# First feed-forward layer of a two-layer decoder trunk: the norm is multiplied into the inputs of later up products, and table steps run in pairs

## Chip, cores and metric

The kernel runs on one core of one Trainium2 chip. The metric is the time of one execution in device microseconds (us). Lower is better.

## What is computed

A trunk of two layers over 512 positions of width 1024, in float32. Each layer has a mixer, a cross-attention into 256 memory tokens and a gated feed-forward part. The change touches the feed-forward part of layer 0 and the tables of the state-space mixer of layer 1, which are worked out beside it. Cut to that:

```
h = rmsnorm(x, g)                       # x * rsqrt(mean(x*x)) * g
up = h @ w_up                           # (512, 1024) @ (1024, 5632)
conv = conv_b + sum_i conv_w[i] * shifted(up, i)     # 3 taps along the positions, causal
val, gate = split(conv, 2)              # 2816 channels each
x = x + (silu(gate) * val) @ w_down     # (512, 2816) @ (2816, 1024)
```

## The kernel before

Activations lie transposed: channels on the 128 partitions, the 512 positions along the free dimension. So the factor rsqrt(mean(x*x)) is one number per column; `rbc` holds it, copied to all partitions, and g is one number per partition.

**Split products.** Every float32 operand is split into a high part that TensorE takes in its faster format and the rest. A product of two operands is three matmuls (`mm3`, lines 207 to 209): high by high, low by high, high by low. The high part is a copy on ScalarE (`copy_hi`, line 113: tiles `wh`, `xh`, `hh`), the low part a subtraction on VectorE (`sub_lo`, line 116: `wl`, `hl`; line 303: `xl`).

**Weights come in chunks.** The stream `W` loads chunks of four 128x128 weight tiles, 12 matmuls each, and splits them. `W.cap[0]` is 4: the chunk in use and three that are ready. `sproj` calls `take` at the start of each chunk:

```
def take(self):
    self.cur = None
    self.fill()                       # splits one more chunk: copy_hi, sub_lo
    hi, lo, self.cur = self.ready.pop(0)
    self.fill()
    return hi, lo
```

So the call for chunk n records the split of chunk n+3, and that split stands in the queues of ScalarE and VectorE at the place in the program where chunk n is taken. Every engine works its queue in that order. The buffers `wh` and `wl` are four deep.

**The feed-forward part** (`ffn_side`) has two halves of 11 columns each. A column j is a round of two up products: the value product j and the gate product NF+j, each of 8 weight tiles, so two chunks and 24 matmuls, into a bank of PSUM named `psup`. The inputs are `xh`, `xl` without the factor `rbc`. After each product `conv` is recorded: VectorE multiplies `psup` by `rbc` into `fu` (line 1454), ScalarE makes the first tap and the bias (`fc`, line 1456), VectorE adds the other two taps (lines 1463 and 1465). After the gate product's `conv`, ScalarE applies SiLU (line 1491, the first time behind the load of its function table); in the next round VectorE multiplies value by gate (line 1460) and the result is split into `hh`, `hl`. In round 0 both convolutions are recorded behind the second product, as `rbc` has to be worked out first (`psst`, `psrow`). After 11 rounds come eight down products `psd` of 33 matmuls, each added into x.

**The table steps.** `ssm_prep` is a generator: each `next(side)` records one step, and `at(n, f)` puts f behind the step that comes n later. `conv` makes one step and each down product five (first half) or three (second half). The steps turn raw matrices on TensorE (`psrw`, four groups of 8 transposes, and `psds`), then build 16 blocks: VectorE ops `bl`, `bt` (lines 640 to 644), a group of 4 transposes `pswi` (line 217) and its copy out; then 16 blocks of `dl`, `bt` (lines 677 to 681) with a group of small float32 matmuls `psk` (line 700), copies `kt` and `wtt`, and DMAs from GpSimd's queue into `tz`. These matmuls and transposes stand between the matmuls of the big products on TensorE.

All PSUM tiles of this stage share one pool of eight banks.

Of the kernel before, what the change touches and what calls it, by code (L numbers as in the profile page):

```python
# [8 lines left out]
F32 = mybir.dt.float32  # L9
# [3 lines left out]
AF = mybir.ActivationFunctionType  # L13
ALU = mybir.AluOpType
# [4 lines left out]
KD = D // 128  # L19
DFF = 2816  # L20
NF = DFF // 128
NH = NF // 2
# [30 lines left out]
def trunk_kernel(  # L53
# [51 lines left out]
    def ttile(name, dt=F32R):  # L105
        return tp.tile([128, 512], dt, tag="t", name=name)
# [125 lines left out]
    def gcol(idx, layer, m):  # L232
        c = goff[idx] + layer * KD + m
        return gcols[:, c:c + 1]
# [335 lines left out]
    def ssm_prep_ops(rg, at):  # L570
# [29 lines left out]
        G.memset(pC[64:128, 0, :], -1.0)  # L600
        G.memset(pCi[:, 0, :], 0.0)

        dsk = rg.tile([64, 16], F32, tag="dsk", name="dsk")
        nc.gpsimd.dma_start(out=dsk, in_=ssm_d[0].rearrange("(g c) -> g c", c=16))
        tzs = [rg.tile([128, 4, 128], F32, tag=f"tz{q}", name="tz") for q in range(2)]
        for t in tzs:
# [7 lines left out]
        ps = psC("psds")  # L614
# [10 lines left out]
        at(6, lambda: cc["turn"](0))  # L625
        at(8, lambda: cc["turn"](8))
        bz = rg.tile([128, 64, 16], F32, tag="bz", name="bz")
        for b in range(2 * NB):
            gs = slice(b * 4, b * 4 + 4)
            sh = [128, 4, 16, 8]  # L630
            big, bt = (hold(n).rearrange("p a b c -> p (a b c)")[:, 0:512].rearrange("p (a b c) -> p a b c", a=4, b=16)
                       for n in ("bl", "bt"))

            def vb(t):
                return t[:, :, gs].rearrange("p c g -> p g c").unsqueeze(3).to_broadcast(sh)

            def vp(t):
                return t[:, 0:8, gs].rearrange("p m g -> p g m").unsqueeze(2).to_broadcast(sh)

            V.tensor_tensor(out=big, in0=vb(b1), in1=vp(pB), op=ALU.mult)  # L640
            yield
            V.tensor_tensor(out=bt, in0=vb(b2), in1=vp(pBi), op=ALU.mult)
            yield
            V.tensor_tensor(out=big, in0=big, in1=bt, op=ALU.add)
            st = {}

            def turn(big=big, st=st):
                st["ps"] = psC("pswi")
                for q in range(4):
                    tr(st["ps"][:, q * 128:(q + 1) * 128], big[:, q].rearrange("p c j -> p (c j)"))  # L650

            def keep(gs=gs, big=big, st=st):
                A.activation(out=bz[:, gs, :], in_=big[:, :, :, 7], func=AF.Copy)
                st["w"] = rg.tile([128, 512], F32, tag="ev", bufs=2, name="wi")
                A.activation(out=st["w"], in_=st["ps"], func=AF.Copy)

            def put(b=b, st=st):
                nc.gpsimd.dma_start(out=d_win[b // 2][:, (b % 2) * 512:(b % 2) * 512 + 512], in_=st["w"])

            at(4, turn)  # L660
            at(5, keep)
            at(6, put)
            yield

        c1, c2 = cc["d"]
        for b in range(2 * NB):
            gs = slice(b * 4, b * 4 + 4)
            sh = [128, 4, 9, 16]
            big, bt = hold("dl"), hold("bt")

            def vb(t):
                return t[:, :, gs].rearrange("p c g -> p g c").unsqueeze(2).to_broadcast(sh)

            def vp(t):
                return t[:, 0:9, gs].rearrange("p m g -> p g m").unsqueeze(3).to_broadcast(sh)

            V.tensor_tensor(out=big, in0=vb(c1), in1=vp(pC), op=ALU.mult)
            yield
            V.tensor_tensor(out=bt, in0=vb(c2), in1=vp(pCi), op=ALU.mult)
            yield  # L680
            V.tensor_tensor(out=big, in0=big, in1=bt, op=ALU.add)
            st = {}

            def d_part(d, b):
                return d[b // 2][:, (b % 2) * 512:(b % 2) * 512 + 512]

            def evw(name):
                return rg.tile([128, 4, 16, 8], F32, tag="ev", bufs=2, name=name)

            def wout(big=big, st=st):  # L690
                st["wo"] = evw("wo")
                A.activation(out=st["wo"], in_=big[:, :, 1:9, :].rearrange("p g j c -> p g c j"), func=AF.Copy)

            def put_wout(b=b, st=st):
                nc.gpsimd.dma_start(out=d_part(d_wout, b), in_=st["wo"].rearrange("p a b c -> p (a b c)"))

            def taps(b=b, big=big, st=st):
                st["ps"] = psC("psk")
                for q in range(4):
                    T.matmul(st["ps"][0:16, q * 128:(q + 1) * 128], lhsT=bz[:, b * 4 + q, :],  # L700
                             rhs=big[:, q, 0:8, :], start=True, stop=True)

            def keep(st=st):
                st["kt"] = rg.tile([16, 4, 8, 16], F32, tag="kt", bufs=1, name="kt")
                A.activation(out=st["kt"].rearrange("p a b c -> p (a b c)"), in_=st["ps"][0:16, :], func=AF.Copy)

            def spread(b=b, gs=gs, st=st):
                kt = st["kt"]
                dd = rg.tile([16, 4, 16], F32, tag="dd", bufs=2, name="dd")
                G.tensor_tensor(out=dd, in0=ident[0:16, 0:16].unsqueeze(1).to_broadcast([16, 4, 16]),  # L710
                                in1=dcol[:, gs].unsqueeze(2).to_broadcast([16, 4, 16]), op=ALU.mult)
                G.tensor_tensor(out=kt[:, :, 0, :], in0=kt[:, :, 0, :], in1=dd, op=ALU.add)  # L712
                ktf = kt.rearrange("p g t c -> p g (t c)")
                for j in range(8):
                    nc.gpsimd.dma_start(out=tzs[b % 2][j:128:8, :, j * 16:128], in_=ktf[:, :, 0:128 - j * 16])  # L715

            def band(b=b, st=st):
                st["wt"] = evw("wtt")
                A.activation(out=st["wt"], in_=tzs[b % 2].rearrange("p g (j c) -> p g c j", j=8), func=AF.Copy)

            def put_band(b=b, st=st):
                nc.gpsimd.dma_start(out=d_part(d_t, b), in_=st["wt"].rearrange("p a b c -> p (a b c)"))

            for n, f in ((2, wout), (3, taps), (3, put_wout), (4, keep), (4, spread), (9, band), (10, put_band)):
                at(n, f)
            yield

# [716 lines left out]
    def ffn_side(rg, layer, norm, hid_extra, nxt, side):  # L1444
# [4 lines left out]
        st = {"n": 0}  # L1449
        wait = {}  # L1450

        def conv(t, ps):
            u = rg.tile([128, 512], F32, tag="fu", bufs=2, name="fu")
            V.tensor_tensor(out=u, in0=ps, in1=st["rbc"], op=ALU.mult)  # L1454
            c = rg.tile([128, 512], F32, tag="fc", bufs=3, name="fc")
            A.activation(out=c, in_=u, func=AF.Identity, scale=cwcol(layer, 2, t), bias=cbcol(layer, t))  # L1456
            gate = wait.pop("gate", None)
            if gate:
                cv, cg, hl = gate
                V.tensor_tensor(out=cv, in0=cv, in1=cg, op=ALU.mult)  # L1460
                copy_hi(hl[0], cv)
            next(side, None)
            V.scalar_tensor_tensor(out=c[:, 1:], in0=u[:, :511], scalar=cwcol(layer, 1, t), in1=c[:, 1:],
                                   op0=ALU.mult, op1=ALU.add)
            V.scalar_tensor_tensor(out=c[:, 2:], in0=u[:, :510], scalar=cwcol(layer, 0, t), in1=c[:, 2:],
                                   op0=ALU.mult, op1=ALU.add)
            if gate:
                sub_lo(hl[1], cv, hl[0])
            return c

        def up(t):
            ps = psB("psup")
            sproj(ps, acts)
            if "rc" not in st:
                st["rc"] = norm.stats_cols()
                st["first"] = ps
                return None
            if "rbc" not in st:
                st["rbc"] = norm_row(st["rc"], 4)
            return ps  # L1480

        for hf in range(2):
            hid = []
            for j in range(hf * NH, (hf + 1) * NH):
                ps = up(j)
                cv = conv(j, ps) if ps is not None else None
                ps = up(NF + j)
                if cv is None:
                    cv = conv(j, st.pop("first"))
                cg = conv(NF + j, ps)  # L1490
                A.activation(out=cg, in_=cg, func=AF.Silu)
                hl = []
                for nm in ("hh", "hl"):
                    if st["n"] % 12 < hid_extra:
                        hl.append(rg.tile([128, 512], F32R, tag="hx", bufs=2 * hid_extra, name=nm))
                    else:
                        hl.append(ttile(nm))
                st["n"] += 1
                hid.append(hl)
                wait["gate"] = (cv, cg, hl)  # L1500
# [352 lines left out]
```

## Time and profile before

| | |
|---|---|
| time, median of 3 runs | 1504.48 us (1503.38 to 1505.69) |
| the profiled execution's own time | 1504.7 us |
| its span, first to last instruction | 1502.9 us |
| mean granted TensorE clock | 0.995 of full speed |
| busy share of the span: TensorE matmul | 99% |
| VectorE, ScalarE, GpSimd | 69%, 49%, 26% |

The profiled execution is one run: 1.8 us of its time lie outside its span, and it stands 0.2 us above the median. Busy matmuls are pipelined: one that is shown as 0.39 us long is followed by the next one 0.23 us later, so what a stage costs TensorE is read from starts, not from durations. The layer-0 feed-forward part runs from 385.7 to about 779.6 us.

### The profile page before, as it was taken

The numbers are of one execution on the slowest core, as the hardware profiler recorded it, in microseconds if no ns is written. First come the engines' busy times: TensorE is split into PE (matmuls) and PEld (weight loads), VectorE is DVE, ScalarE is ACT, GpSimd is POOL, SyncE is SP. The second block draws the span as 40 slices with busy tenths as digits, with TensorE's granted clock in tenths as the row PEclk, the third lists the DMA queues.
The fourth block names the chain that finished last, engine by engine and source line by source line (L and its number), as shares of the span: only waits on it lengthen the run. The fifth ranks groups of instructions, "written<-read, shape, count | busy, mean of one in ns | idle before, by whom it ended". The sixth has DMA issues, their size and how long they took to land.

```text
span 1502.9 us, 21036 instructions
## 1 busy us (share of the span) xinstructions
PE 1480.7 (99%) x7347; PEld 1234.6 (82%) x7347; DVE 1029.8 (69%) x1607; ACT 735.1 (49%) x1303; POOL 394.8 (26%) x823
## 2 busy tenths in 40 slices
PE   9999999999999999999999999999999999999998
PEld 7887888888888887888788988888888888888887
DVE  4776676676588897888865666556567775377755
ACT  5566673344445534555663545434444443245533
POOL 7864119998000013333752120000000000000002
PEclk9999999999999999999999999999999999999999
DMA  5313253324433344444568876332133333333331
GB/s 182 97 46 101 64 155 103 114 85 123 115 100 99 115 151 142 127 122 132 157 192 306 263 250 190 105 99 70 57 91 92 99 95 94 100 98 98 94 117 56
DMA packets 271941, 183.99 MB, mean 122 GB/s; under 512 B 21271, under 2 KB 252763, under 8 KB 271835
## 3 DMA queue, kind: packets, MB, share of 16 engines
q1 hardware_dynamic: 244731, 132.79, 30.2%
q0 software_dynamic: 15872, 42.26, 8.3%
q10 hardware_dynamic: 11232, 7.61, 1.6%
q8 instruction: 57, 0.93, 0.3%
q14 instruction: 49, 0.40, 0.1%
HBM read 156.13 MB, written 24.12 MB: 120 GB/s over the span
## 4 chain that ended last, share of the span: by engine, by line
PE 86%; DVE 5%; ACT 3%; DMA 2%; issue 2%; SPq 0%; ACTq 0%; POOL 0%; DVEq 0%; POOLq 0%
PE psup L207 10%; PE psup L208 10%; PE psup L209 10%; PE psd L207 5%; PE psd L209 5%; PE psd L208 5%; PE pso L209 2%; PE pso L208 2%; PE pso L207 2%; PE psg L208 2%; PE psg L207 2%; PE psg L209 2%; PE psq L207 2%; PE psq L209 2%; PE psq L208 2%
## 5 line engine op out<-in xcount | busy, mean ns | idle before, releaser
L116 DVE TENSOR_TENSOR wl<-wr,wh 128x512 fp32r<-128x512 f32 (+2 forms) x467 | 325.6, 713 | 141.6 <-ACT wh L113 140.7
L113 ACT ACTIVATE wh<-wr 128x512 fp32r<-128x512 f32 (+2 forms) x467 | 280.7, 617 | 248.3 <-PE psup L208 84.6
L207 PE MATMUL psup<-xh,wh 128*128 128x512 f32 x704 | 275.7, 392 | 0.0
L208 PE MATMUL psup<-xl,wh 128*128 128x512 f32 x704 | 274.4, 390 | 0.0
L209 PE MATMUL psup<-xh,wl 128*128 128x512 f32 x704 | 274.1, 389 | 0.0
L207 PEld LDWEIGHTS psup<-xh,wh 128*128 128x128 f32 x704 | 132.1, 188 | 28.8 <-issue 1.5
L1542 POOL TENSOR_TENSOR acc<-acc,sq 128x256 f32<-128x256 f32 x12 | 8.8, 734 | 558.2 <-ACT sq L1540 558.1
L209 PEld LDWEIGHTS psup<-xh,wl 128*128 128x128 f32 x704 | 132.1, 188 | 27.9 <-DVE wl L116 0.3
L208 PEld LDWEIGHTS psup<-xl,wh 128*128 128x128 f32 x704 | 132.2, 188 | 27.2 <-issue 0.2
L207 PE MATMUL psd<-hh,wh 128*128 128x512 f32 x328 | 130.5, 398 | 0.0
L209 PE MATMUL psd<-hh,wl 128*128 128x512 f32 x328 | 128.3, 391 | 0.0
L208 PE MATMUL psd<-hl,wh 128*128 128x512 f32 x328 | 127.9, 390 | 0.2 <-DVE hl L116 0.2
L1456 ACT ACTIVATE fc<-fu,ccols 128x512 f32<-128x512 f32 x44 | 35.9, 817 | 93.6 <-DVE fu L1454 93.6
L302 ACT ACTIVATE xh<-xT,gcols 128x512 fp32r<-128x512 f32 x40 | 33.4, 835 | 97.4 <-DVE xT L325 69.1
L207 PEld LDWEIGHTS psd<-hh,wh 128*128 128x128 f32 x328 | 61.6, 188 | 14.5 <-issue 1.5
L209 PEld LDWEIGHTS psd<-hh,wl 128*128 128x128 f32 x328 | 61.5, 188 | 13.6
L208 PEld LDWEIGHTS psd<-hl,wh 128*128 128x128 f32 x328 | 61.6, 188 | 13.0 <-DVE hl L116 0.5
L715 POOL DMA_DIRECT2D tz<-kt x128 | 65.1, 516 | 7.4 <-POOL kt L712 4.7
L303 DVE SCALAR_TENSOR_TENSOR xl<-xT,gcols,xh 128x512 fp32r<-128x512 f32 x40 | 34.7, 869 | 33.7 <-ACT xh L302 33.5
L207 PE MATMUL psq<-xh,wh 128*128 128x512 f32 x128 | 51.1, 399 | 0.0
L1401 DVE TENSOR_TENSOR fu<-psup,rbc 128x512 f32<-128x512 f32 x44 | 30.3, 688 | 29.4 <-PE psup L209 28.1
L207 PE MATMUL pso<-oh,wh 128*128 128x512 f32 x128 | 50.0, 391 | 0.0
(351 smaller groups left out, 3439.7 us busy)
## 6 DMA issues: line engine op xcount, KB each, us to landing
wr<-in_ffn_w_up_dram SPq DMA_DIRECT2D x176, 256.0 KB, 3.0
wr<-in_ffn_w_down_dram SPq DMA_DIRECT2D x70, 256.0 KB, 2.9
wr<-in_xa_w_kv_dram SPq DMA_DIRECT2D x64, 256.0 KB, 3.7
wr<-in_ab_w_in_dram SPq DMA_DIRECT2D x32, 256.0 KB, 2.8
wr<-in_xa_w_q_dram SPq DMA_DIRECT2D x32, 256.0 KB, 2.9
wr<-in_xa_w_o_dram SPq DMA_DIRECT2D x32, 256.0 KB, 2.9
wr<-in_ssm_w_glu_dram SPq DMA_DIRECT2D x29, 256.0 KB, 2.9
wr<-in_ffn_w_down_dram SPq DMA_DIRECT2D x24, 192.0 KB, 2.6
```

The source lines that it names most:

```text
L113: A.activation(out=o, in_=i, func=AF.Copy)
L116: V.tensor_tensor(out=o, in0=i, in1=hi.bitcast(F32), op=ALU.subtract)
L207: T.matmul(ps, lhsT=lh, rhs=rh, start=first, stop=False)
L208: T.matmul(ps, lhsT=lh, rhs=rl, start=False, stop=False)
L209: T.matmul(ps, lhsT=ll, rhs=rh, start=False, stop=last)
L302: A.activation(out=ho, in_=src, func=AF.Copy, scale=g)
L303: V.scalar_tensor_tensor(out=lo, in0=src, scalar=g, in1=ho.bitcast(F32), op0=ALU.mult, op1=ALU.subtract)
L715: nc.gpsimd.dma_start(out=tzs[b % 2][j:128:8, :, j * 16:128], in_=ktf[:, :, 0:128 - j * 16])
L1401: V.tensor_tensor(out=u, in0=ps, in1=rbc, op=ALU.mult)
L1456: A.activation(out=c, in_=u, func=AF.Identity, scale=cwcol(layer, 2, t), bias=cbcol(layer, t))
L1542: G.tensor_tensor(out=acc[:, sl], in0=acc[:, sl], in1=sq[:, 0:256], op=ALU.add)
```

## The change

Rounds 0 to 4 (`NU` = 5) of the first half keep the old inputs. In rounds 0 to 3, `scale_acts` makes one new input tile ahead of the gate product's convolution and one behind it: VectorE multiplies a tile of x by `rbc` (`xn`, in the buffers of `fu`), ScalarE makes `xh` from it, VectorE `xl`. All later up products, of both halves, take these eight, and their convolutions read the bank of PSUM directly, without `fu`. The first six convolutions make no table step; from round 5 of the first half on, the convolution of the gate product makes two. The four-transpose groups of two blocks are put next to each other, with their copies and DMAs, and so are the `psk` groups of two blocks. The tile `dsk` is given 64 columns of which 16 are used (256 bytes for each partition in place of 64).

```diff
-        dsk = rg.tile([64, 16], F32, tag="dsk", name="dsk")
+        dsk = rg.tile([64, 64], F32, tag="dsk", name="dsk")[:, 0:16]
...
-            at(4, turn)
-            at(5, keep)
-            at(6, put)
+            pair.append((turn, keep, put))
+            if b % 2:
+                for n in range(3):
+                    for fs in pair:
+                        at(3 + n, fs[n])
+                pair = []
...
-            for n, f in ((2, wout), (3, taps), (3, put_wout), (4, keep), (4, spread), (9, band), (10, put_band)):
+            o = 3 - 3 * (b % 2)
+            for n, f in ((2, wout), (3, put_wout), (3 + o, taps), (4 + 3 * (b % 2) + o, keep),
+                         (4 + 3 * (b % 2) + o, spread), (9 + 3 * (b % 2) + o, band), (10 + 3 * (b % 2) + o, put_band)):
...
+        scaled = []
+        NU = 5
+        def scale_acts(n):
+            for m in range(len(scaled), min(KD, len(scaled) + n)):
+                g = gcol(norm.idx, norm.layer, m)
+                xn = rg.tile([128, 512], F32, tag="fu", bufs=2, name="xn")
+                V.tensor_tensor(out=xn, in0=xT[m], in1=st["rbc"], op=ALU.mult)
+                h, l = ttile("xh"), ttile("xl")
+                A.activation(out=h, in_=xn, func=AF.Copy, scale=g)
+                V.scalar_tensor_tensor(out=l, in0=xn, scalar=g, in1=h.bitcast(F32), op0=ALU.mult, op1=ALU.subtract)
+                scaled.append((h, l))
...
-            u = rg.tile([128, 512], F32, tag="fu", bufs=2, name="fu")
-            V.tensor_tensor(out=u, in0=ps, in1=st["rbc"], op=ALU.mult)
+            if st["n"] < NU:
+                u = rg.tile([128, 512], F32, tag="fu", bufs=2, name="fu")
+                V.tensor_tensor(out=u, in0=ps, in1=st["rbc"], op=ALU.mult)
+            else:
+                u = ps
...
-            next(side, None)
+            for _ in range(0 if st["n"] < 3 else 2 if st["n"] < NH and st["n"] >= NU and t >= NF else 1):
+                next(side, None)
...
-            sproj(ps, acts)
+            sproj(ps, acts if st["n"] < NU else scaled)
...
+                if st["n"] < NU - 1:
+                    scale_acts(1)
                 cg = conv(NF + j, ps)
+                if st["n"] < NU - 1:
+                    scale_acts(1)
                 A.activation(out=cg, in_=cg, func=AF.Silu)
```

What this does to the queues is shown at three places. The first is ScalarE in round 0 of the first half, from the copy of `rbc` to the split of two weight chunks. Before:

```order
L282 ACTIVATE rbc<-psrow 128x512
L1456 ACTIVATE fc<-fu,ccols 128x512 x2
L1491 ACT_TABLE_LOAD
L1491 ACTIVATE fc<-fc 128x512
L113 ACTIVATE wh<-wr 128x512 x2
```

With the change:

```order
L282 ACTIVATE rbc<-psrow 128x512
L1480 ACTIVATE fc<-fu,ccols 128x512
L1469 ACTIVATE xh<-xn,gcols 128x512
L1480 ACTIVATE fc<-fu,ccols 128x512
L1469 ACTIVATE xh<-xn,gcols 128x512
L1520 ACT_TABLE_LOAD
L1520 ACTIVATE fc<-fc 128x512
L113 ACTIVATE wh<-wr 128x512 x2
```

Two copies `xh` now stand ahead of the two `wh`, the second of them also ahead of SiLU and its table.

The second place is VectorE in the same round, from the first multiplication by `rbc` to the low parts of the same two chunks. Before:

```order
L1454 TENSOR_TENSOR fu<-psup,rbc 128x512
L1463 SCALAR_TENSOR_TENSOR fc<-fu,ccols,fc 128x511
L1465 SCALAR_TENSOR_TENSOR fc<-fu,ccols,fc 128x510
L1454 TENSOR_TENSOR fu<-psup,rbc 128x512
L1463 SCALAR_TENSOR_TENSOR fc<-fu,ccols,fc 128x511
L1465 SCALAR_TENSOR_TENSOR fc<-fu,ccols,fc 128x510
L116 TENSOR_TENSOR wl<-wr,wh 128x512 x2
```

With the change:

```order
L1476 TENSOR_TENSOR fu<-psup,rbc 128x512
L1488 SCALAR_TENSOR_TENSOR fc<-fu,ccols,fc 128x511
L1490 SCALAR_TENSOR_TENSOR fc<-fu,ccols,fc 128x510
L1467 TENSOR_TENSOR xn<-xT_78,rbc 128x512
L1470 SCALAR_TENSOR_TENSOR xl<-xn,gcols,xh 128x512
L1476 TENSOR_TENSOR fu<-psup,rbc 128x512
L1488 SCALAR_TENSOR_TENSOR fc<-fu,ccols,fc 128x511
L1490 SCALAR_TENSOR_TENSOR fc<-fu,ccols,fc 128x510
L1467 TENSOR_TENSOR xn<-xT_79,rbc 128x512
L1470 SCALAR_TENSOR_TENSOR xl<-xn,gcols,xh 128x512
L116 TENSOR_TENSOR wl<-wr,wh 128x512 x2
```

Four instructions are new; each `xl` waits for the `xh` that ScalarE makes of the `xn` just ahead of it. The same two pairs stand in rounds 1, 2 and 3.

The third place is TensorE, where a block's `psk` group stands between two matmuls of a big product. Before, at 16 places:

```order
L208 MATMUL psup<-xl,wh 128x512
L209 MATMUL psup<-xh,wl 128x512
L700 MATMUL psk<-dl,bz 16x128 x4
L207 MATMUL psup<-xh,wh 128x512
L208 MATMUL psup<-xl,wh 128x512
```

With the change, at eight:

```order
L208 MATMUL psup<-xl,wh 128x512
L209 MATMUL psup<-xh,wl 128x512
L704 MATMUL psk<-dl,bz 16x128 x8
L207 MATMUL psup<-xh,wh 128x512
L208 MATMUL psup<-xl,wh 128x512
```

The groups `pswi` change in the same way, from 16 places of 4 to eight of 8. The two first groups `psrw`, which stood ahead of products 2 and 3 (rounds counted from 0, two products each), now stand ahead of products 8 and 9.

## Rows read from the trace of the kernel before

**Rows 1.** Page: busy time, share of the span and instructions of each engine

```profile
PE 1480.7 (99%) x7347; PEld 1234.6 (82%) x7347; DVE 1029.8 (69%) x1607; ACT 735.1 (49%) x1303; POOL 394.8 (26%) x823
```

**Rows 2.** Timeline of TensorE, products 0 to 3: start us, length us, instruction

```profile
385.74 0.39 PE L207 MATMUL psup<-xh,wh 128*128 128x512 f32 x1
...
391.18 0.95 PE L316 MATMUL psst<-ones,acc 128*128 128x1 f32 x8
...
398.51 1.09 PE L217 MATMUL psrw<-cs,raw 64*128 64x64 f32 x8
399.53 0.50 PE L207 MATMUL psup<-xh,wh 128*128 128x512 f32 x1
...
406.30 0.50 PE L207 MATMUL psup<-xh,wh 128*128 128x512 f32 x1
```

**Rows 3.** Timeline of ScalarE in round 0; in brackets idle time before, and releaser

```profile
405.51 1.28 ACT L1491 ACT_TABLE_LOAD   x1 [1.65 <-DVE fc L1465]
...
407.35 1.14 ACT L113 ACTIVATE wh<-wr 128x512 fp32r<-128x512 f32 x2
```

**Rows 4.** Timeline of VectorE in rounds 0 to 2

```profile
402.33 0.68 DVE L1454 TENSOR_TENSOR fu<-psup,rbc 128x512 f32<-128x512 f32 x1
...
404.69 0.75 DVE L1465 SCALAR_TENSOR_TENSOR fc<-fu,ccols,fc 128x510 f32<-128x510 f32 x1
...
409.20 0.68 DVE L1454 TENSOR_TENSOR fu<-psup,rbc 128x512 f32<-128x512 f32 x1
...
410.77 0.75 DVE L1463 SCALAR_TENSOR_TENSOR fc<-fu,ccols,fc 128x511 f32<-128x511 f32 x1 [0.29 <-ACT fc L1456]
...
419.44 1.29 DVE L116 TENSOR_TENSOR wl<-wr,wh 128x512 fp32r<-128x512 f32 x2 [1.42 <-ACT wh L113]
420.65 0.68 DVE L1454 TENSOR_TENSOR fu<-psup,rbc 128x512 f32<-128x512 f32 x1
...
422.90 0.75 DVE L1463 SCALAR_TENSOR_TENSOR fc<-fu,ccols,fc 128x511 f32<-128x511 f32 x1
...
430.62 1.29 DVE L116 TENSOR_TENSOR wl<-wr,wh 128x512 fp32r<-128x512 f32 x2 [1.28 <-ACT wh L113]
```

**Rows 5.** Timeline of all engines, 385.7 to 388.9 us: making one input tile

```profile
385.93 0.69 DVE L325 TENSOR_TENSOR xT<-xT,pso 128x512 f32<-128x512 f32 x1 [1.41 <-PE pso L209]
...
386.66 0.73 ACT L302 ACTIVATE xh<-xT,gcols 128x512 fp32r<-128x512 f32 x1 [0.27 <-DVE xT L325]
387.29 0.61 ACT L310 ACTIVATE sq<-xT 128x512 f32<-128x512 f32 x1
387.42 0.75 DVE L303 SCALAR_TENSOR_TENSOR xl<-xT,gcols,xh 128x512 fp32r<-128x512 f32 x1 [0.19 <-ACT xh L302]
388.08 0.69 DVE L311 TENSOR_TENSOR acc<-acc,sq 128x512 f32<-128x512 f32 x1
```

**Rows 6.** Timeline of TensorE around one psk group

```profile
593.24 0.39 PE L209 MATMUL psup<-xh,wl 128*128 128x512 f32 x1
593.55 1.05 PE L700 MATMUL psk<-dl,bz 128*16 128x128 f32 x8
...
597.15 0.39 PE L209 MATMUL psup<-xh,wl 128*128 128x512 f32 x1
```

**Rows 7.** Timeline of TensorE around one pswi group

```profile
485.14 0.39 PE L209 MATMUL psup<-xh,wl 128*128 128x512 f32 x1
485.37 0.60 PE L217 MATMUL pswi<-cs,bl 128*128 128x128 f32 x4
...
488.33 0.39 PE L209 MATMUL psup<-xh,wl 128*128 128x512 f32 x1
```

**Rows 8.** Groups by line and shape: busy us, mean ns, idle before

```profile
L1113 DVE SCALAR_TENSOR_TENSOR sa<-psz,sa 128x512 f32<-128x512 f32 x16 | 11.0, 690 | 9.6 <-ACT sa L1107 9.6
```

**Rows 9.** Stretches: busy us of PE, PEld, DVE, ACT, POOL; PEclk, DMA share, GB/s

```profile
814.00:818.00 4.00, 1.59 (x15) 1.45 (x13) 2.58 (x4) 0.88 (x3) 1.68 (x4) 1.00 0.97 378
818.00:822.00 4.00, 4.00 (x25) 4.00 (x25) 2.83 (x4) 2.66 (x5) 0.41 (x1) 0.62 0.98 369
```

More of the change, by code (lines that the diff above doesn't have):

```diff
@@ L658, in put @@
                 nc.gpsimd.dma_start(out=d_win[b // 2][:, (b % 2) * 512:(b % 2) * 512 + 512], in_=st["w"])
-            at(4, turn)
-            at(5, keep)
-            at(6, put)
+            pair.append((turn, keep, put))
[3 more added lines that the diff above has]
+                        at(3 + n, fs[n])
+                pair = []
             yield
```

## Prediction

> **What bounds the kernel now.** I read the page's shares first: TensorE is busy 99% of the span, VectorE 69%, ScalarE less [rows 1]. So a change gains only what it takes off TensorE, or loses what TensorE is made to wait. Next comes TensorE's timeline at the start of the stage [rows 2], for its pace: the first up product begins at 385.74 us and what follows its 24 matmuls at 391.18, so a 128x512 matmul costs 5.44/24 = 0.2267 us. A chunk of 12 is 2.72 us, a product 5.44, a round of value and gate 10.88.
>
> Then I read the timelines of ScalarE and VectorE [rows 3, 4] for how close they run to TensorE. Number the chunks from 0, so product p uses chunks 2p and 2p+1. Taking chunk n records the split of chunk n+3, so the splits of chunks 7 and 8 are recorded when product 2 takes chunks 4 and 5. In round 0 they stand in ScalarE's queue behind both first convolutions and SiLU. The pair `wh` starts at 407.35 [rows 3]; its first is done half of its 1.14 later, at about 407.9. Product 3 starts at 406.30 [rows 2] and needs chunk 7 after one chunk, at 409.02. The margin is about 1.1 us. That is the number to watch, since the change puts work just ahead of these splits.
>
> **The first stall.** In round 0 the change does two things against that margin.
>
> TensorE comes earlier: the first `psrw` group (1.02 us by the starts, 398.51 to 399.53 [rows 2]) is gone from there. Product 2 starts at 398.51, product 3 at 403.95, and chunk 7 is needed at 406.67.
>
> The split comes later, since `scale_acts` goes back and forth between VectorE and ScalarE. The nearest rows are those that make an input tile from `xT` at the stage's start [rows 5]: VectorE's multiplication starts at 385.93, ScalarE's `xh` 0.73 later, VectorE's `xl` 1.49 later, VectorE's next instruction 0.66 after that; ScalarE's next is 0.63 behind `xh`. VectorE thus loses 1.49 + 0.66 = 2.15 us for a tile that it waits through. The second `fu` and all behind it move back by 2.15. The last tap stands at 404.69 [rows 4], now at 406.84; 0.66 later, at 407.50, the second `xn` starts, `xh` at 408.23, and ScalarE is free for SiLU's table at 408.86. Before, that load started at 405.51 [rows 3]. So SiLU and the splits move by 3.35 us: `wh` of chunk 7 starts at 410.70 and is done at about 411.3. TensorE waits from 406.67 for 4.65 us; the third matmul wants `wl` as well, which starts behind `wh` and runs 0.65 [rows 4], while two matmuls cover 0.45: some 0.25 more. **First stall: 4.9 us.**
>
> **Rounds 1 to 4.** A stall resets the margin to about zero, so from here the round of VectorE and ScalarE counts against TensorE's 10.88. From the pair `wl` at 419.44 to the one at 430.62 is 11.18 [rows 4]. That round holds two table steps, which the change takes out of rounds 0 to 2. One of them lies in the chain: from `fu` to the next tap is 22.90 − 20.65 = 2.25 us with it and 10.77 − 9.20 = 1.57 without. The other lies in VectorE's wait for `fc`. A bare round is 11.18 − 0.68 = 10.50.
>
> The scaling adds 2.15 for the first tile. For the second, SiLU starts 0.66 + 0.73 + 0.63 = 2.02 behind the start of the last tap, where 0.82 was the delay before (404.69 to 405.51 [rows 3, 4]): 1.20. A round is 13.85, and TensorE, which needs 10.88, waits 2.9 us in each of rounds 1 and 2. In round 3, two moved `psrw` groups give TensorE 1.02 and 1.09 us of other work, and 0.9 is left. In round 4 there is no scaling, but ScalarE again makes the copies of `psrw`; from the lists of its work I estimate 0.6. From round 5 on `fu` is gone from VectorE and its chain is shorter than before. **Rounds together: 2 × 2.9 + 0.9 + 0.6 = 7.3; all stalls 12.2 us.**
>
> **What pairing saves.** A `psk` group of one block takes 3.91 us from a matmul to the one 12 later (593.24 to 597.15 [rows 6]); less 2.72 it costs 1.19. Its eight recorded matmuls last 1.05 and four transposes of the same width 0.60 [rows 7], so each takes (1.05 − 0.60)/4 = 0.11 and eight 0.89. The rest, 0.30, is the change to small matmuls and back. It is paid once less for each of eight pairs: 2.4 us. A `pswi` group costs 488.33 − 485.14 − 2.72 = 0.47 [rows 7], of which four transposes at 0.11 are 0.44: merging saves 0.03, times eight is 0.2. Other groups that now stand side by side, and `psk` groups among down products, I put at 0.6. **Saving: 3.2 us**; its bounds are zero (the change-over is paid for each block anyway) and 16 × 0.30 = 4.8.
>
> **Costed at nothing.** The convolution that reads PSUM: VectorE's tap from PSUM has a mean of 690 ns [rows 8], from SBUF 0.75 [rows 4], so the row gives no loss; the bank stays occupied while three readers pass, where one passed before, but there are eight banks, and a product fills one in 5.44. If taps from PSUM were slower by as much as a tenth, that is 0.15 us for each convolution, against the 0.68 of a removed `fu`. The Trainium skill (Perfetto Trace Analysis, Optimizing Scalar/DVE Operations) gives VectorE about 60 ns of overhead for an instruction on SBUF and about 125 on PSUM; as an estimate from that page two taps would lose 0.13 us a product, and the sum would not move, as VectorE is not what TensorE waits for from round 5 on. The trace of this kernel shows no such loss. The 34 removed `fu` free some 23 us on VectorE, which is worth nothing to TensorE where it doesn't wait for VectorE. The wider `dsk` moves the buffers behind it; its own transfer is one, long ahead of its use. Nothing on TensorE's path waits for GpSimd, 26% busy [rows 1], which issues the moved DMAs; if these came late, the next layer's mixer would show it. I take zero for both.
>
> **Sum.** 12.2 − 3.2 = +9.0. The profiled run's own time is 1504.7 us, 0.2 above the median; with 9.0 it is **1513.7 us**. Its own range, by ±25% of the stalls (3.1) and the saving's bounds (1.6 below, 3.2 above), is 1509 to 1519.
>
> **The rivals.** *The clock falls too* (0.15). At 814 to 818 us TensorE is busy 1.59 of 4 us, and in the next 4 us the granted clock is 0.62 with TensorE busy throughout [rows 9]: a wait of about 2.4 us was followed by matmuls at the lower of two levels (1.2 and 2.4 GHz). Here five waits follow one another. Where TensorE waits for the chain anyway, slow matmuls cost nothing; behind the last long wait they do. As (1 − 0.62) × 4 = 1.5 us are lost in those 4 us, I take this to go on for 6.8 us at half clock, which loses 3.4: 1517.1. The Trainium skill (TensorE: Matmul & The Clock Gate, What's actually happening) says that the gate lets a share of the clock's pulses through by the engine's recent activity; that agrees with these rows. Whether these waits, with matmuls between, do it is open.
>
> *Only the first stall remains* (0.07). If the two engines catch up in rounds 1 to 3, because ScalarE and VectorE overlap better there than in round 0, the time is 1504.7 + 4.9 − 3.2 = 1506.4, within the 0.2% (3.0 us) that a measurement of this kernel can tell from no change. Against it: in 13.85 us there is no gap that shrinks when they hurry, since each `xl` waits for its own `xh`.
>
> *The scaling is hidden* (0.08), the case on the other side. VectorE idles 1.42 and 1.28 us a round waiting for `wh` [rows 4], and if tiles are worked out in those gaps with splits on time, only the saving is left: 1501.5, faster by 0.2%. It decides at one point: `wh` of chunk 7 must start by about 406.0, ahead of 406.67. The order speaks against it, with `xn`, `xh` and `xl` ahead of these splits in both queues.
>
> *Pairing doesn't do what it says* (0.05): the change to small matmuls costs the same per block, 1504.7 + 12.2 = 1516.9.
>
> **How the numbers follow.** The forecast has 0.65, and its range is given above. All rivals but two are slower. Range of 8 in 10: I leave out the two fast cases (0.15) and reach to 1518.5 above and 1508.5 below, the latter for a saving of 4.8 with stalls of 8.6. Faster by over 0.2%: 0.08; within: 0.07; slower: 0.85.
>
> **What would show it.** In the changed kernel's timeline TensorE would wait some 4.7 us for `wh` of ScalarE near 406.7, then 2.5 to 3 in the next two rounds, and about 1 in the fourth; the pair `wh` would start near 410.7, with ScalarE's table load at 408.9. `psk` groups of 16 matmuls would stand between matmuls of the big products and cost about 2.1 us where two cost 2.4. VectorE's `fu` would fall from 44 to ten in this layer. The forecast is wrong if `wh` there starts before 406.7; if idle time of TensorE in rounds 0 to 4 is far from 12; if the granted clock falls behind round 2; or if the matmuls behind round 5 take longer than before, which would point at readers of PSUM that hold banks.

## Result and the profile after

The changed kernel takes 1513.47 us (median, 1513.0 to 1514.84) where the kernel before takes 1504.18: ratio 1.0057, 95% interval 1.0045 to 1.0069, 9.3 us slower. 9.0 was forecast. The profiled execution has a span of 1511.6 us, 8.7 more than before. Its busy shares read almost as before [rows 1]:

```profile
PE 1480.8 (98%) x7347; PEld 1236.9 (82%) x7347; DVE 1021.6 (68%) x1589; ACT 740.4 (49%) x1311; POOL 397.0 (26%) x823
```

TensorE is as long busy as before, in a longer span: most of the difference is waiting. (Busy time also holds matmuls at a lower clock, shown below, and lacks what pairing saved.) TensorE's waits in the stage (engine, line, what it waited for: us in all, times, longest):

```profile
PE psup L207 <- ACT wh L113: 7.0, 2, 4.7
PE pswi L217 <- DVE bl L645: 0.5, 1, 0.5
```

TensorE's timeline shows where (start, length, in brackets the idle time before it):

```profile
386.01 0.39 PE L207 MATMUL psup<-xh,wh 128*128 128x512 f32 x1
...
406.67 0.39 PE L209 MATMUL psup<-xh,wl 128*128 128x512 f32 x1
411.73 0.80 PE L207 MATMUL psup<-xh,wh 128*128 128x512 f32 x1 [4.67 <-ACT wh L113]
...
417.80 0.39 PE L209 MATMUL psup<-xh,wl 128*128 128x512 f32 x1
...
439.28 0.50 PE L207 MATMUL psup<-xh,wh 128*128 128x512 f32 x1 [2.33 <-ACT wh L113]
...
525.49 0.39 PE L207 MATMUL psd<-hh,wh 128*128 128x512 f32 x1
...
787.32 0.39 PE L209 MATMUL psd<-hh,wl 128*128 128x512 f32 x1
```

The first wait is chunk 7, at the place and of the size that were worked out (4.65). What led to it, on ScalarE:

```profile
409.23 1.28 ACT L1520 ACT_TABLE_LOAD   x1
...
411.06 1.13 ACT L113 ACTIVATE wh<-wr 128x512 fp32r<-128x512 f32 x2
```

and on VectorE:

```profile
402.61 0.68 DVE L1467 TENSOR_TENSOR xn<-xT,rbc 128x512 f32<-128x512 f32 x1
404.08 0.75 DVE L1470 SCALAR_TENSOR_TENSOR xl<-xn,gcols,xh 128x512 fp32r<-128x512 f32 x1 [0.79 <-ACT xh L1469]
404.75 0.68 DVE L1476 TENSOR_TENSOR fu<-psup,rbc 128x512 f32<-128x512 f32 x1
...
411.70 1.29 DVE L116 TENSOR_TENSOR wl<-wr,wh 128x512 fp32r<-128x512 f32 x2 [1.71 <-ACT wh L113]
...
425.48 1.29 DVE L116 TENSOR_TENSOR wl<-wr,wh 128x512 fp32r<-128x512 f32 x2 [0.29 <-ACT wh L113]
...
439.26 1.29 DVE L116 TENSOR_TENSOR wl<-wr,wh 128x512 fp32r<-128x512 f32 x2 [0.29 <-ACT wh L113]
```

From `xn` to the next `fu` is 2.14 us (2.15 forecast); this execution runs 0.27 later than that of before, so 409.23 answers to 408.86 and 411.06 to 410.70. A round is 425.48 − 411.70 = 13.78, twice in a row (13.85 forecast). But between 411.7 and 439 TensorE waits only once, not twice. The stretches say why (busy us of PE, PEld, DVE, ACT, POOL; granted clock; DMA share; GB/s):

```profile
406.90:411.70 4.80, 0.15 (x1) 0.00 (x0) 2.27 (x4) 3.18 (x5) 0.00 (x0) 0.92 0.00 0
411.70:417.60 5.90, 5.88 (x14) 4.58 (x15) 5.58 (x9) 2.87 (x5) 0.00 (x0) 0.50 0.30 89
417.60:430.00 12.40, 12.40 (x55) 9.78 (x54) 9.22 (x15) 6.20 (x10) 0.00 (x0) 1.00 0.29 86
```

After the wait the clock was granted at 0.50, the lower level (1.2 GHz), for 5.9 us. Fourteen matmuls, from 411.73 to 417.80, took 6.07 us, where fourteen at 0.2267 take 3.17: 2.9 us more. That filled the gap of 2.9 that round 1 had been forecast to wait.

A `psk` group in the changed kernel, with the starts of the products around it:

```profile
615.27 0.39 PE L207 MATMUL psup<-xh,wh 128*128 128x512 f32 x1
...
620.80 1.92 PE L704 MATMUL psk<-dl,bz 128*16 128x128 f32 x16
...
628.23 0.39 PE L207 MATMUL psup<-xh,wh 128*128 128x512 f32 x1
```

Two products take 12.96 us where 48 matmuls take 10.88: the pair costs 2.08, two single groups 2 × 1.19 = 2.38 [rows 6]. The forecast was 2.1.

**An account of the stage.** For each profiled execution I took the distance from the first matmul of product 0 to the first down product and to the stage's last down matmul, and subtracted that of before. Of before these rows belong to it, with 385.74 [rows 2]:

```profile
513.53 0.40 PE L207 MATMUL psd<-hh,wh 128*128 128x512 f32 x1
...
779.42 0.39 PE L209 MATMUL psd<-hh,wl 128*128 128x512 f32 x1
```

The changed kernel has lost 11.7 us at the first down product (12.2 forecast for all stalls) and 7.6 at the end: 4.1 come back (3.2 forecast). The same for all runs; times are medians, each beside that of the kernel before measured along with it:

| run | time, before | ratio (95%) | at first down | at end of stage |
|---|---|---|---|---|
| changed kernel | 1513.47, 1504.18 | 1.0057 (1.0045 to 1.0069) | +11.7 | +7.6 |
| pairs only | 1505.77, 1504.70 | 1.0002 (0.9992 to 1.0012) | −0.1 | +0.5 |
| scaling, wider `dsk`, no pairs | 1516.53, 1504.70 | 1.0073 (1.0058 to 1.0088) | +13.1 | +11.3 |
| scaling on GpSimd | 1512.78, 1504.70 | 1.0040 (1.0023 to 1.0057) | +10.8 | +6.7 |
| scaling interleaved | 1506.00, 1504.70 | 1.0004 (0.9995 to 1.0013) | +3.3 | −0.6 |
| wider `dsk` only | 1503.83, 1505.11 | 0.9992 (0.9983 to 1.0000) | −0.1 | −1.0 |
| matmuls in the wait | 1515.30, 1505.11 | 1.0067 (1.0049 to 1.0085) | +11.7 | +7.8 |
| `psup` copied | 1524.06, 1505.11 | 1.0127 (1.0113 to 1.0142) | +15.0 | +16.6 |
| `dsk` and spaced pairs | 1503.17, 1505.11 | 0.9986 (0.9978 to 0.9995) | −0.1 | −3.1 |
| no scaling | 1510.39, 1504.75 | 1.0030 (1.0019 to 1.0042) | +1.9 | +5.9 |
| single steps | 1513.51, 1504.75 | 1.0051 (1.0032 to 1.0070) | +13.0 | +8.4 |
| late `xl` | 1505.24, 1504.75 | 0.9998 (0.9987 to 1.0009) | +3.5 | −0.2 |

One of the five runs with GpSimd, at 1642.7 us with a mean clock of 0.85, was disturbed and is not in its row. The stage's account is of one execution; it is sharper than the times, which scatter by 2 to 8 us and also hold what lies outside the stage.

The same account by stretches shows where each part gains and loses (us more than before, from the first matmul of one stretch to that of the next):

| run | first half: up | first half: down | second half: up | second half: down |
|---|---|---|---|---|
| changed kernel | +11.69 | −1.03 | −2.18 | −0.85 |
| scaling, wider `dsk`, no pairs | +13.11 | −1.05 | 0.00 | −0.75 |
| wider `dsk` only | −0.05 | −0.21 | 0.00 | −0.75 |
| pairs only | −0.06 | +1.63 | −2.18 | +1.12 |
| `dsk` and spaced pairs | −0.07 | −1.57 | −2.18 | +0.75 |
| single steps | +12.95 | −1.55 | −2.18 | −0.83 |
| no scaling | +1.93 | +3.60 | −2.18 | +2.50 |

The second half's up products are 2.18 us shorter in all ten profiles with pairs and unchanged in the two others. Before, seven `psk` groups stand there, in the changed kernel three pairs: 7 × 1.19 − 3 × 2.08 = 2.1. Of that, 0.9 is saved; the rest is one block's group, which has moved into the down products.

### The profile page after: what moved, and what is told of

It is laid out like the page before. It is cut to its first block, busy times and chain, and to the rows that moved or that the text cites. A ratio compares the mean times of both kernels' runs of the same rounds, so it can differ in the third digit from the quotient of the medians.

```text
span 1511.6 us, 20993 instructions
## 1 busy us (share of the span) xinstructions
PE 1480.8 (98%) x7347; PEld 1236.9 (82%) x7347; DVE 1021.6 (68%) x1589; ACT 740.4 (49%) x1311; POOL 397.0 (26%) x823
## 4 chain that ended last, share of the span: by engine, by line
PE 78%; DVE 9%; ACT 5%; issue 3%; DMA 2%; POOL 1%; SPq 0%; ACTq 0%; DVEq 0%; POOLq 0%
PE psup L207 9%; PE psup L209 9%; PE psup L208 9%; PE psd L207 4%; PE psd L209 4%; PE psd L208 4%; DVE wl L116 2%; PE pso L208 2%; PE pso L209 2%; PE pso L207 2%; PE psg L209 2%; PE psg L208 2%; PE psg L207 2%; PE psq L207 2%; PE psq L209 2%
## 5 line engine op out<-in xcount | busy, mean ns | idle before, releaser
L208 PEld LDWEIGHTS psd<-hl,wh 128*128 128x128 f32 x328 | 61.6, 188 | 12.4
L209 PE MATMUL psq<-xh,wl 128*128 128x512 f32 x128 | 49.9, 390 | 0.0
```

The lines of the kernel that those rows point to most:

```text
L208: T.matmul(ps, lhsT=lh, rhs=rl, start=False, stop=False)
L209: T.matmul(ps, lhsT=ll, rhs=rh, start=False, stop=last)
```

## The experiments

My theory was that of the prediction: the scaling goes back and forth between VectorE and ScalarE ahead of the weight splits, and TensorE waits for these; pairs give a little back. The main rivals: table steps that were moved make the loss, the busy time of VectorE does, or the clock.

**The parts alone.** The kernel before with the pairing alone (shown for the `pswi` groups; the line that orders the `psk` steps is that of the change too):

```diff
+            pair.append((turn, keep, put))
+            if b % 2:
+                for n in range(3):
+                    for fs in pair:
+                        at(3 + n, fs[n])
+                pair = []
```

> The kernel before with the pairing of the pswi and psk groups alone: one table step for each convolution as before, no scaled inputs, fu everywhere. Theory (the stalls come from the scaling, the pairs save about 3.4 us of TensorE): no new stall in rounds 0 to 4, 1500.8 us (1500 to 1501.8). Rival (a pair costs what two single groups cost): 1504.2. Rival (the later, denser table work of pairs makes a wait of its own): above 1504.2.

Measured: no change. The 2.2 us saved in the second half's up products are eaten by the down products of both halves (+1.6 and +1.1), where the denser steps make waits that were not there before. TensorE's waits in the stage:

```profile
PE pswi L217 <- DVE bl L645: 1.1, 1, 1.1
PE psd L207 <- ACT hh L113: 0.7, 1, 0.7
```

The second of two `pswi` groups comes one step sooner after its `bl` than a single one did (3 for 4). So the second rival's wait is there, though the time shows no change.

The kernel before with scaled inputs and convolutions from PSUM, but single groups and one step for each convolution. This kernel also has the wider `dsk`, which the expectation leaves out:

> The kernel before with the scaled inputs and the convolution that reads PSUM, but single groups and one table step for each convolution as before. Theory (the round of VectorE and ScalarE gets 3.35 us longer in four rounds, 13.4 us, less the margin of 1.1, plus what the table steps add): 1517 us (1515.5 to 1519), with waits for wh in rounds 0 to 4. Rival (the scaling costs only the measured net of 9.3 us and the pairs save nothing): 1513.5. Rival (most of the loss comes from table steps that were moved, which are back here): below 1510.

Measured +13.1 at the first down product, 1516.5: the number is the theory's. Its sum is another: three waits, and behind the last of them, of 2.94 us, matmuls at the lower clock. TensorE's waits, and the stretch behind the last:

```profile
PE psup L207 <- ACT wh L113: 6.7, 3, 2.9
```

```profile
441.09:447.00 5.91, 5.91 (x14) 4.61 (x15) 5.88 (x10) 2.86 (x5) 0.00 (x0) 0.50 0.31 89
```

What the lower clock costs in this kernel is not separated from what TensorE would have waited anyway.

The changed kernel with only the table steps put back to one for each convolution:

```diff
-            for _ in range(0 if st["n"] < 3 else 2 if st["n"] < NH and st["n"] >= NU and t >= NF else 1):
-                next(side, None)
+            next(side, None)
```

> The changed kernel with one table step for each convolution from the first on, as before; scaling, PSUM reads, pairs and dsk as in the changed kernel. Theory (moving the steps neither hides nor makes the stall; the scaling gives 13.1 us as in the run with the scaling alone, pairs and dsk take 4.1): 1513.7 us (1512 to 1515.5). Rival (the steps had to leave the first rounds for the scaling to fit at all): 1517 or more.

Measured 1513.5, and +13.0 at the first down product for 11.7: the moved steps don't make the loss, and leaving the first rounds saves 1.3 us of it. They do shift it between rounds: here the four waits are 2.1, 2.9, 3.0 and 1.0 us, where the changed kernel has 4.7 and 2.3.

**Order or busy time.** The same 24 instructions in the same rounds, written into the convolutions; `xl` stands behind the last tap, and `xn` has buffers of its own:

```diff
+            xl = scale_acts() if len(scaled) < KD else None   # xn, xh
             gate = wait.pop("gate", None)
...
+            if xl:
+                xl()
             return c
```

> The changed kernel with the same 24 scaling instructions on the same engines in the same rounds, but written into the convolutions: xn behind fu, where VectorE waits for fc, xh behind fc, and xl behind the last tap. Theory (the back and forth between the two engines is what costs, not the busy time): a tile adds about 1.0 us to a round in the value convolution and nothing in the gate convolution; first wait about 2.2 us, then 0.6 a round, 1504.5 us (1503 to 1506.5). Rival (VectorE's busy time in these rounds is what counts, and it is the same): 1513.5.

TensorE waits once, for 1.9 us, and the stage ends 0.6 us sooner than before. VectorE's pairs `wl`, one round apart:

```profile
408.72 1.29 DVE L116 TENSOR_TENSOR wl<-wr,wh 128x512 fp32r<-128x512 f32 x2 [1.89 <-ACT wh L113]
...
420.09 1.29 DVE L116 TENSOR_TENSOR wl<-wr,wh 128x512 fp32r<-128x512 f32 x2 [0.62 <-ACT wh L113]
...
431.47 1.29 DVE L116 TENSOR_TENSOR wl<-wr,wh 128x512 fp32r<-128x512 f32 x2 [0.62 <-ACT wh L113]
```

A round is 11.4 us, where the changed kernel's is 13.78. VectorE is busy for about as long in both (third number, changed kernel first), so 2.4 us a round were latency:

```profile
425.48:439.26 13.78, 11.47 (x49) 8.85 (x48) 10.61 (x16) 6.20 (x11) 0.00 (x0) 1.00 0.26 77
```

```profile
420.09:431.47 11.38, 11.38 (x49) 8.86 (x48) 10.34 (x17) 6.10 (x11) 0.00 (x0) 1.00 0.32 94
```

The buffers are a second difference, but in the changed kernel VectorE waits in these rounds only for `xh`, `fc` and `wh` of ScalarE, never for a buffer. The time, 1506.0 in ten runs from 1503.8 to 1507.7, is within the expected range and shows no difference from before.

Then both `xl` of a round go behind the gate convolution's last tap, where VectorE waits for `wh`, with single steps and spaced pairs:

```diff
+            while xls and t >= NF:
+                xls.pop(0)()
             return c
```

> The interleaved scaling with both low parts of a round behind the gate convolution's last tap, where VectorE waits for SiLU and wh (1.4 us a round), and one table step for each convolution as before; PSUM reads, pairs with their transposes one step later, wider dsk. Theory (scaling is hidden when each of its instructions stands where its engine waits anyway): about 1 us of waits in rounds 0 to 4, less 4.1 and the 0.9 us of late waits that the run with pairs and dsk has, 1500.5 us (1499.5 to 1502.5), not slower than that run. Rival (the margin of 1.1 us can't take the table steps and the scaling together): waits of 3 us or more, 1503.5.

This expectation failed: 3.5 us are lost by the first down product. VectorE's pairs `wl` again:

```profile
420.21 1.29 DVE L116 TENSOR_TENSOR wl<-wr,wh 128x512 fp32r<-128x512 f32 x2 [0.71 <-ACT wh L113]
...
432.60 1.29 DVE L116 TENSOR_TENSOR wl<-wr,wh 128x512 fp32r<-128x512 f32 x2
...
444.53 1.29 DVE L116 TENSOR_TENSOR wl<-wr,wh 128x512 fp32r<-128x512 f32 x2
```

and the stretch between two of them:

```profile
420.21:432.60 12.39, 11.76 (x48) 8.78 (x48) 12.32 (x19) 6.10 (x11) 0.00 (x0) 1.00 0.29 85
```

The idle time ahead of them, 1.24 us a round earlier, goes to nothing as the table operations begin; rounds are 12.4 and 11.9 us, above 10.88, and VectorE is busy for 12.32 of the 12.39. With the latency gone, VectorE's busy time is what counts: I had given the same idle 1.4 us to the scaling and to the table steps.

The arithmetic on GpSimd (`xn` times g in two operations, made one tile ahead, then `xl`), `xh` on ScalarE as before:

```diff
+                G.tensor_tensor(out=xn, in0=xT[m], in1=st["rbc"], op=ALU.mult)
+                G.tensor_scalar(out=xn, in0=xn, scalar1=gcol(norm.idx, norm.layer, m), scalar2=None, op0=ALU.mult)
...
+            copy_hi(h, xn)
+            G.tensor_tensor(out=l, in0=xn, in1=h.bitcast(F32), op=ALU.subtract)
```

> The changed kernel with the multiplication by rbc and by g and the low part on GpSimd, so that only the copy to xh is left on ScalarE and nothing on VectorE. Theory (TensorE waits because these instructions stand ahead of the weight splits in VectorE's queue): the wait for chunk 7 falls from 4.7 to about 1.5 us (what the two moved psrw groups no longer cover), no waits behind it, 1502.3 us (1501 to 1504). Rival (it is the work as such, GpSimd is too slow for two tiles a round or slows VectorE): waits again, 1507 or more.

The rival came true: +10.8. Groups of VectorE from 400 to 450 us in this run, and for `wl` the changed kernel's (busy us, mean ns):

```profile
L116 DVE TENSOR_TENSOR wl<-wr,wh 128x512 fp32r<-128x512 f32 x12 | 14.0, 1207 | 5.3 <-ACT wh L113 5.3
...
L1486 DVE TENSOR_TENSOR fu<-psup,rbc 128x512 f32<-128x512 f32 x8 | 5.4, 681 | 2.5 <-issue 2.5
```

```profile
L116 DVE TENSOR_TENSOR wl<-wr,wh 128x512 fp32r<-128x512 f32 x12 | 7.7, 686 | 2.3 <-ACT wh L113 2.3
```

GpSimd's operations take 1.3 to 2.4 us each, and while they run VectorE's `wl` takes 1207 ns for 686, but `fu`, with one of its inputs in PSUM, 681. The Trainium skill (SBUF — State Buffer, SBUF: two separate sides) says that GpSimd and a VectorE operation with two SBUF inputs lock each other out of a shared port pair; these rows agree, and I should have weighed it ahead of the run. Whether GpSimd is also too slow by itself, the rival's other half, this run doesn't separate.

**The clock.** The changed kernel with 20 more matmuls, into a bank that nobody reads, between chunks 6 and 7:

```diff
+                        for q in range(20):
+                            T.matmul(pd, lhsT=acts[0][0][:, 0:128], rhs=acts[0][0], start=True, stop=True)
```

> The changed kernel with 20 more matmuls of 128x512 (4.5 us) between chunk 6 and chunk 7, where TensorE waits 4.7 us; they write a bank that nobody reads. Theory (the fall of the clock behind this wait costs nothing, because TensorE waits for wh again a round later): no fall of the clock there, the 2.7 us that the slow matmuls took turn into an idle wait in round 1, 1513.5 us (1512.5 to 1514.5). Rival (the clock is part of the loss): 1510.8.

The same three stretches in this run:

```profile
406.90:411.70 4.80, 4.80 (x23) 3.97 (x22) 3.09 (x5) 1.94 (x3) 0.00 (x0) 1.00 0.00 0
411.70:417.60 5.90, 5.75 (x24) 4.13 (x23) 3.87 (x7) 4.45 (x8) 0.00 (x0) 1.00 0.29 86
417.60:430.00 12.40, 10.10 (x43) 7.73 (x43) 9.55 (x15) 4.82 (x8) 0.00 (x0) 1.00 0.18 52
```

The clock stays at 1.00, and 2.3 us of idle time appear in the third stretch. The stage ends at +7.8, against +7.6: in this kernel the lower clock cost nothing. The median, 1515.3, lies above the expected range; the profiled execution lost 4.3 us after the stage, and why is open.

**What was costed at nothing.** The kernel before with the wider `dsk` alone (the diff's first line):

> The kernel before with the wider dsk alone, nothing else. In the traces so far the matmuls of the down products that read the first hidden tiles follow one another at 229 to 235 ns with the narrow dsk and at 227 ns in every run with the wide one, which is about 1.8 us over 16 down products. Theory (the wider tile shifts hh and hl of the first rounds to another address, and TensorE reads them faster there): 1.8 us less, 1502.7 us (1501.7 to 1503.5), 227 ns in all down products. Rival (the difference comes from the removed fu, from less work on VectorE): no change, 229 to 235 ns as before.

The stage gets 1.0 us shorter, 0.75 of it in the second half's down products and only 0.2 in the first half's; the theory had all down products at the same pace. The first matmul of the second and of the third down product of the second half, before:

```profile
719.43 0.39 PE L207 MATMUL psd<-hh,wh 128*128 128x512 f32 x1
...
728.21 0.39 PE L207 MATMUL psd<-hh,wh 128*128 128x512 f32 x1
```

and with the wider `dsk`:

```profile
719.45 0.39 PE L207 MATMUL psd<-hh,wh 128*128 128x512 f32 x1
...
728.13 0.39 PE L207 MATMUL psd<-hh,wh 128*128 128x512 f32 x1
```

8.78 and 8.68 us with the same work between, and so in each of the eight. That the width does it is shown; that the shifted addresses of `hh` and `hl` do is the likely reading, which I have not tried with another shift. The time agrees in sign, its interval touching no change. The 1.8 us that I expected were too many.

The changed kernel with `psup` copied to `fu` by VectorE in the later rounds:

```diff
-                u = ps
+                u = rg.tile([128, 512], F32, tag="fu", bufs=2, name="fu")
+                V.tensor_copy(out=u, in_=ps)
```

> The changed kernel with psup copied to fu by VectorE ahead of the convolution in the later rounds, so that no convolution reads PSUM directly. Theory (reading PSUM directly is off TensorE's path both ways): 1513.5 us (1512.5 to 1514.5), down products at 227 ns as in the changed kernel. Rival (VectorE's load, not the address, sets the pace of the down products): they fall back to 229 to 235 ns, 1515.3.

The expectation failed, by 10.6 us, some 9 of which are lost by the end of the stage. And the changed kernel without scaled inputs (`fu` everywhere, the calls of `scale_acts` gone):

```diff
-            if st["n"] < NU:
+            if True:
...
-            sproj(ps, acts if st["n"] < NU else scaled)
+            sproj(ps, acts)
```

> The changed kernel without the scaled inputs: all products take the old inputs and every convolution multiplies by rbc into fu; the table steps, the pairs and the wider dsk as in the changed kernel. Theory (the copy of psup with VectorE cost 9 us because from round 5 on two more table operations a round stand in VectorE's queue, and the removed fu made room for them): a wait of about 1.5 us in round 0, none to round 4, then the waits of late rounds again, 1510 us (1508 to 1512.5). Rival (those waits only came because the scaling had used up the margin): no late waits, 1501.5.

1510.4, as expected. Its waits in the stage:

```profile
PE psd L207 <- ACT hh L113: 2.6, 1, 2.6
PE psd L209 <- DVE wl L116: 1.6, 3, 0.7
PE psup L207 <- ACT wh L113: 1.2, 1, 1.2
```

From round 5 the changed kernel makes three table steps a round. With `fu` still in VectorE's queue, the hidden tiles are late when the down products begin. VectorE's last taps of two gate convolutions, one round apart, at the end of the first half:

```profile
510.25 0.75 DVE L1490 SCALAR_TENSOR_TENSOR fc<-fu,ccols,fc 128x510 f32<-128x510 f32 x1
...
522.05 0.75 DVE L1490 SCALAR_TENSOR_TENSOR fc<-fu,ccols,fc 128x510 f32<-128x510 f32 x1
```

That is 11.8 us, as in most rounds from round 5 on, and more than the 10.88 of TensorE's products; in the changed kernel these rounds are 10.6 to 10.8, but for one of 12.1. So removing `fu` was worth 9 us here, most of it against a burden that the change itself had brought: it takes 8.0 us off the down products of both halves (changed kernel against no scaling). With pairs and single steps it is some 4 us (single steps against pairs only, less what `dsk` gives), and without pairs 0.8 (scaling against wider `dsk` only). These differences are worked out from the table of stretches; no run has `fu` removed and nothing else.

Most of the 0.8 lies in the first down product. There TensorE waits before, and not in the run with scaling and no pairs; the matmul ahead of this one started 0.72 us earlier, where 0.23 is the rule:

```profile
522.11 0.50 PE L208 MATMUL psd<-hl,wh 128*128 128x512 f32 x1 [0.22 <-DVE hl L116]
```

By the starts that product takes 9.17 us before, 9.20 with the wider `dsk` alone and 8.44 in the run with scaling.

**The parts that pay.** The kernel before with the wider `dsk` and the pairs, transposes at `at(4 + n, ...)`:

> The kernel before with the wider dsk and the pairs, without scaled inputs; the transposes of a pair are put one step later than in the run with the pairs alone, where they waited for bl of VectorE (1.1 us) and what followed them late (1.5 us). Theory: the pairs save about 3 us when they don't wait, the address 1.8, 1499.5 us (1498.5 to 1501). Rival (the pair's denser work on ScalarE and VectorE in the first half's down products makes waits wherever it is put): 1502.5.

The stage ends 3.1 us sooner, the span is 1500.0 us, and the ratio 0.9986 (0.9978 to 0.9995) is clear of 1: 0.14% faster than before, the fastest kernel here, though not by the 4.7 us expected. `dsk` gives 1.0, which leaves 2.1 for the pairs; two waits remain:

```profile
PE psd L209 <- DVE wl L116: 0.9, 2, 0.7
PE psrow L275 <- DVE dg L267: 0.4, 1, 0.4
```

## Why the prediction came out right, and where its steps didn't

- **The sum**: the stage lost 7.6 us for the 9.0 of the forecast. Stalls were 0.5 smaller and the saving 0.9 larger than worked out. That the time came within 0.2 us of the forecast is partly luck: the profiled execution lost 1.1 us more outside the stage, where other runs lost anything from −0.7 to 4.3 behind it.
- **The first stall** (4.9): 4.7 us idle, through the steps as written. Confirmed by the order: interleaved, the wait is 1.9 us.
- **Rounds 1 to 4** (7.3): the round was 13.78 for 13.85. By the first down product 11.7 us were lost for 12.2. The forecast's own sign, idle time of about 12 in rounds 0 to 4, isn't met: only 7.0 are idle. Another 2.9 are the slow matmuls; the rest lies in pieces too small for the view of waits, such as spread matmuls behind a wait.
- **The clock rival**: its mechanism was there, its price was not. The clock did fall after the first wait, and the slow matmuls lay where TensorE would have waited. The filled wait shows it. The 6.8 us that this rival reckons with are those of the kernel before, where the granted clock is 0.73, 0.50, 0.50 and 0.56 in the four stretches of 2 us from 818 us; here it was 5.9.
- **Pairing** (3.2): a pair saves 0.30 us as worked out. But of the 4.1 that came back, 1.8 come back without pairs too, in the run with scaling and the wider `dsk`. So pairs gave 2.3: about eight times 0.30, without the 0.8 that I had added for other groups. Of the 1.8, the wider `dsk` alone gives 1.0, and 0.8 goes with the removed `fu`. I put both at zero, and these were the steps mis-sized: of `dsk` I looked for who waits for it and not for what it shifts.
- **PSUM reads at nothing**: the rows bear out the price of an instruction. Changed kernel, taps from PSUM and from SBUF (busy us, mean ns):

```profile
L1490 DVE SCALAR_TENSOR_TENSOR fc<-psup,ccols,fc 128x510 f32<-128x510 f32 x34 | 25.4, 749 | 1.2
...
L1490 DVE SCALAR_TENSOR_TENSOR fc<-fu,ccols,fc 128x510 f32<-128x510 f32 x10 | 7.5, 750 | 0.4
```

  The Trainium skill (Perfetto Trace Analysis, Optimizing Scalar/DVE Operations) gives about 60 ns of overhead on SBUF and about 125 on PSUM; these two means, 749 and 750 ns, show no such difference. But "worth nothing to TensorE" failed: I didn't ask what else had been put into the queue that `fu` left, nor whether a hidden tile was already late before.
- **The hidden-scaling rival** was wrong for the order as written, and came close with another order.

## What to carry to other kernels

Where a tile is made by two engines in turn, count what each engine waits, not what it is busy: here 2.4 us of 13.8 a round were latency that another order of the same instructions took away. An edit costed at nothing needs two questions: what cover does it use, and does another part of the same change use it too? Take a change apart before judging it: the wider `dsk` with pairs one step later made a kernel 0.14% faster than before, where the whole change made one 0.6% slower. And compare the parts stretch by stretch: a saving in one can hide a wait in another.

## What I had not expected of the hardware

- The granted clock fell to 0.50 for 5.9 us after a wait of 4.67 us, but stayed at 1.00 after one of 2.33 in the same kernel. In the run with scaling and no pairs it fell after a wait of 2.15 (0.63 in the next 4 us), and with single steps it stayed at 1.00 after one of 2.90: the length of the wait alone doesn't tell. In the kernel before, it fell after a busy time of 1.59 in 4 us [rows 9].
- GpSimd's work stretched VectorE's subtraction `wl`, on two SBUF tiles, from 686 to 1207 ns and left the multiplication `fu`, with an input in PSUM, at 681.
- A tile of 48 more unused columns made each down product of the second half about 0.1 us faster.
